# Differential attention: the head norms' sums of squares from split squares, in two passes over a constant tile

## The chip, the cores and the metric

One core of one Trainium2 chip runs the whole program. The metric is the device time of one execution in microseconds (us), lower is better. The engines named below are TensorE (PE; its weight loads are shown as PEld), VectorE (DVE), ScalarE (ACT), GpSimd (POOL) and SyncE (SP). Each takes its instructions from a list of its own, and a semaphore makes one engine wait for another.

## The reference

Two blocks of layers run over 512 positions of width 1024, with 16 meta tokens ahead of them (528 in all). The first block is a stick-breaking attention, an MLP, a differential attention and an MLP; the second holds another attention, a recurrent layer and a mixture of experts. The change lies in the differential attention alone. Its 8 heads have two keys and two queries of 64 rows each and a value of 128 rows, and every one of them, and the output too, goes through a root-mean-square norm:

```python
def rmsnorm(x, g):
    xf = x.astype(jnp.float32)
    y = xf * lax.rsqrt(jnp.mean(xf * xf, axis=-1, keepdims=True) + EPS)
    return (y * g.astype(jnp.float32)).astype(x.dtype)
...
k1 = apply_partial_rope(rmsnorm(kk[..., 0, :], kv_k_norm_g[0]), cos, sin)
q1 = apply_partial_rope(rmsnorm(qq[..., 0, :], b_q_norm_g[j, 0]), cos, sin)
w = probs(q1b, k1f) - lam * probs(q2b, k2f)     # two softmaxes, causal
o = rmsnorm(o, b_subln_g[j]) * (1.0 - lam_init)
h = h + merge_heads(o).astype(h.dtype) @ b_w_o[j]
```

The mean of squares over a head's rows is the sum that the change is about.

## The kernel before

Activations lie with the feature on the partition and the position on the free axis. A dense product in full precision is written as three matmuls of the type F32R, on operands that are split into a high and a low part (`hi*whi`, `lo*whi`, `hi*wlo`; lines 215 to 217). The method `split` (lines 367 to 369) makes such a pair from an fp32 tile: ScalarE copies to the high part, VectorE subtracts it from the tile.

The differential attention works on one head ("pair": its two keys, its two queries) after another, eight in all. Two Python generators are interleaved by `script`. `df_dense` yields the dense products: keys (two halves of 264 columns), queries and values of pair p, and at last a part of the output product. `df_attn` yields the attention of the pairs: scores (`z`, line 867), softmax, the transposes of its weights (`flip`, lines 902 to 907), the product with the values (line 974) and the norm of the output (`tail`, lines 981 to 988). The tables PAT, PAT6 and PAT7 say how many dense steps stand between the steps of the attention; so TensorE's order is written by hand, and the other engines' order is chosen by a scheduler from dependencies and priorities.

A norm runs so. `head_square` (line 749) squares a head's 128 rows on ScalarE into a tile `hsq`. `head_norm` (lines 752 to 764) multiplies `hsq` on TensorE by `blk`, a 128x128 tile with 1/64 in two diagonal blocks, so that the means of both 64-row heads stand on all their rows (line 758: two halves of 264 columns for keys, 512 for queries). `rsqrt` (lines 345 to 357) then needs ScalarE four times (349, 353, 354, 355) and VectorE twice (356, 357). Lines 760 to 764 apply gain and rotary embedding on VectorE, with one product on POOL (line 763). The `due` list in `df_dense` says after how many dense steps the norm of keys and of queries is emitted (DK 4, DQ 1; for the first pair D0). The sums go to the PSUM pool `dn`, of two banks, which the dense products use too. The norm of the output does the same with `osq` (line 979) and `ones_s`, filled with 1/128 (line 983); its result is split into `oT_hi` and `oT_lo`.

The names in rows: `dn`, `z`, `tr`, `o` are PSUM tiles; `wT` holds the transposed weights; `e` the exponentials; `st` the maxima and sums of a softmax; `k` and `dfq`, `dfl` the split keys and queries; `ms` the mean square; `hrs` and `ors` the reciprocal roots.

Of the kernel before, what the change touches and what calls it, by code (L numbers as in the profile page):

```python
# [7 lines left out]
F32 = mybir.dt.float32  # L8
F32R = mybir.dt.float32r
# [10 lines left out]
S = 512  # L20
L = S + NM
# [8 lines left out]
class Net:  # L30
# [682 lines left out]

    def df_setup(self):
        nc, c = self.nc, self.ap
        self.blk = c.tile([128, 128], F32, name="blk")
        nc.vector.memset(self.blk, 0.0)
        for r in (slice(0, 64), slice(64, 128)):
            nc.vector.memset(self.blk[r, r], 1.0 / 64)
        self.ones_s = c.tile([128, 128], F32, name="ones_s")  # L720
        nc.vector.memset(self.ones_s, 1.0 / 128)
        self.rope = c.tile([128, 2, L], F32, name="rope")
        nc.sync.dma_start(self.rope, self.w["rope"])
        self.small = c.tile([128, 3], F32, name="bsmall")
        nc.sync.dma_start(self.small, self.w["b_small"])
        nc.vector.tensor_scalar(self.small[:, 0:1], self.small[:, 0:1], -0.5, None, op0=ALU.mult)
        nc.vector.tensor_scalar(self.small[:, 1:2], self.small[:, 1:2], -0.5 * 0.125, None, op0=ALU.mult)
        lam_init = 0.8 - 0.6 * math.exp(-0.3)
        nc.vector.tensor_scalar(self.small[:, 2:3], self.small[:, 2:3], -0.5 * (1.0 - lam_init), None, op0=ALU.mult)
        lp = c.tile([128, 4, 64], F32, name="lp")  # L730
        src = self.w["b_lambda"]
        nc.sync.dma_start(lp, bass.AP(tensor=src.tensor, offset=src.offset, ap=[[0, 128], [64, 4], [1, 64]]))
        pr = c.tile([128, L], F32, name="hsq", bufs=2)[:, :64]
        lam = c.tile([128, 2], F32, name="lam")
        for i in range(2):
            nc.vector.scalar_tensor_tensor(pr, lp[:, 2 * i, :], 1.0, lp[:, 2 * i + 1, :], op0=ALU.mult, op1=ALU.mult,
                                           accum_out=lam[:, i:i + 1])
        nc.scalar.activation(lam, lam, AF.Exp)
        self.ql = self.lows(c, "dfl", S, 3)
        self.meta_rows(c, 1)  # L740
        self.nlam = c.tile([128, 1], F32, name="nlam")
        nc.vector.tensor_sub(self.nlam, lam[:, 1:2], lam[:, 0:1])
        nc.vector.tensor_scalar(self.nlam, self.nlam, -lam_init, None, op0=ALU.add)
# [3 lines left out]
    def head_square(self, x):  # L747
        sq = self.ap.tile([128, L], F32, name="hsq", bufs=2)[:, :x.shape[1]]
        self.nc.scalar.activation(sq, x, AF.Square)
        return sq  # L750

    def head_norm(self, x, sq, c0, g):

        nc, n = self.nc, x.shape[1]
        rs = self.ap.tile([128, L], F32, name="hrs")[:, :n]
        for a, b in (HALVES if n == L else ((0, n),)):
            ps = self.bank(b - a)
            nc.tensor.matmul(ps, self.blk, sq[:, a:b], start=True, stop=True)
            self.rsqrt(rs[:, a:b], ps, b - a)
        nc.vector.scalar_tensor_tensor(x, x, g, rs, op0=ALU.mult, op1=ALU.mult)  # L760
        nc.vector.stream_shuffle(sq, x, self.SHUF)
        nc.vector.tensor_mul(x, x, self.rope[:, 0, c0:c0 + n])
        nc.gpsimd.tensor_mul(sq, sq, self.rope[:, 1, c0:c0 + n])
        nc.vector.tensor_add(x, x, sq)
# [146 lines left out]
    def df_attn(self, o_pairs):  # L911
        nc, ap = self.nc, self.ap
# [14 lines left out]
        w, tail = {}, None  # L927
# [14 lines left out]
        for p in range(8):  # L942
# [7 lines left out]
            if tail:  # L950
                tail()
# [21 lines left out]
            for i, j in enumerate((4, 0, 1, 2, 3)):  # L973
                nc.tensor.matmul(o[:, 128 * (j % 4):], vn[:, j, :], wT[:, j, 128 * (j % 4):], start=(i == 0),
                                 stop=(i == 4), skip_group_check=True)
            of = ap.tile([128, S], F32, name="of", bufs=2)
            nc.scalar.activation(of, o, AF.Copy)
            sq = ap.tile([128, S], F32, name="osq")
            nc.scalar.activation(sq, of, AF.Square)

            def tail(p=p, of=of, sq=sq):
                pn = self.bank()
                nc.tensor.matmul(pn, self.ones_s, sq, start=True, stop=True)
                rs = ap.tile([128, S], F32, name="ors")
                self.rsqrt(rs, pn, S)
                nc.vector.scalar_tensor_tensor(of, of, gain, rs, op0=ALU.mult, op1=ALU.mult)
                self.split(of, *o_pairs[p][:2])
                self.outs = p + 1
        yield self.END[0]
        tail()  # L990
        yield self.END[1]

# [1166 lines left out]
```

## Time and profile before

| | |
|---|---|
| median of 3 runs | 2514.88 us (2513.75 to 2515.01) |
| profiled execution | 2519.67 us, of which the span is 2517.9 us |
| granted TensorE clock, mean | 0.987 of full speed |
| PE busy | 2425.6 us, 96% of the span |
| DVE busy | 1449.4 us, 58% |
| ACT busy | 1167.3 us, 46% |
| POOL busy | 164.8 us, 7% |
| differential attention | from about 720 to 990 us of the span |
| one pair in its steady part | 29.75 us (a pair's first key sum at 777.25, the next at 807.02) |

The busy shares are means over the program; within a stage the waits tell more. A row of a timeline gives the start, the duration, the engine, the line, the tiles, the number of instructions, and in brackets the idle time ahead of it and what ended it. A matmul's duration holds its way through the array, so successive starts tell what it occupies.

### The profile page before, as it was taken

To read this page: it belongs to the slowest core of one execution; us is meant where nothing else is said; L and a number is where in the kernel's file an instruction comes from. 1 tells how busy PE (TensorE), PEld (TensorE's weight loads), DVE (VectorE), ACT (ScalarE), POOL (GpSimd) and SP (SyncE) were. 2 spreads that over 40 slices of the span, in tenths; PEclk is the share of its full clock that TensorE was granted. 3 is DMA by queue.
4 is the path that set the end of the run, shared out by engine and by line. 5 is a ranking of instruction groups with operands and counts; after the bars stand their busy time and mean duration, and the time that the engine had idled before them with its cause. 6 is when DMAs were issued, how large, how long until landed. Compare 5 with 4: busy or idle time off the path is not lost. (4 is left out here: it accounts for less than half of the span.)

```text
span 2517.9 us, 38327 instructions
## 1 busy us (share of the span) xinstructions
PE 2425.6 (96%) x14656; PEld 1937.2 (77%) x14656; DVE 1449.4 (58%) x2744; ACT 1167.3 (46%) x2271; POOL 164.8 (7%) x169
## 2 busy tenths in 40 slices
PE   8999988999999999999999999999999989999996
PEld 8999988999988887788887888999888733344332
DVE  6666686443457776533445658899654544344434
ACT  6777653332447776422334666555653322222222
POOL 0000055000001110000000000000000111000000
PEclk9999999999999999999999999999999889999998
DMA  3111299333342223333334212222245799997996
GB/s 119 51 51 35 69 343 378 122 93 88 102 154 101 101 101 97 105 97 92 94 99 120 73 57 62 68 59 64 80 129 205 282 380 409 408 401 300 408 407 240
DMA packets 126986, 418.26 MB, mean 166 GB/s; under 512 B 16464, under 2 KB 20816, under 8 KB 126800
## 3 DMA queue, kind: packets, MB, share of 16 engines
q1 hardware_dynamic: 116288, 382.22, 43.2%
q0 software_dynamic: 9936, 31.47, 3.2%
q8 instruction: 116, 1.90, 0.3%
q10 hardware_dynamic: 576, 2.10, 0.2%
q14 instruction: 70, 0.57, 0.1%
HBM read 386.83 MB, written 33.62 MB: 167 GB/s over the span
## 5 line engine op out<-in xcount | busy, mean ns | idle before, releaser
L215 PE MATMUL dn<-hg_hi,whi 128*128 128x264 f32 (+1 forms) x1616 | 525.0, 325 | 8.7 <-ACT hg_hi L336 6.9
L182 ACT ACTIVATE whi<-wraw 128x1024 fp32r<-128x1024 f32 (+1 forms) x261 | 259.1, 993 | 551.1 <-PE dn L216 266.1
L217 PE MATMUL dn<-hg_hi,wlo 128*128 128x264 f32 (+1 forms) x1616 | 511.2, 316 | 3.0 <-DVE wlo L183 3.0
L216 PE MATMUL dn<-hg_lo,whi 128*128 128x264 f32 (+1 forms) x1616 | 510.7, 316 | 2.1 <-DVE hg_lo L337 2.0
L183 DVE TENSOR_TENSOR wlo<-wraw,whi 128x1024 fp32r<-128x1024 f32 (+1 forms) x261 | 300.1, 1150 | 77.4 <-ACT whi L182 75.9
L215 PEld LDWEIGHTS dn<-hg_hi,whi 128*128 128x128 f32 x1616 | 308.2, 191 | 30.1 <-ACT hg_hi L336 6.9
L216 PEld LDWEIGHTS dn<-hg_lo,whi 128*128 128x128 f32 x1616 | 308.0, 191 | 24.1 <-DVE hg_lo L337 4.3
L217 PEld LDWEIGHTS dn<-hg_hi,wlo 128*128 128x128 f32 x1616 | 307.9, 191 | 21.5 <-DVE wlo L183 3.3
L1839 PE MATMUL b<-ew,X 128*64 128x512 f32 (+1 forms) x964 | 236.4, 595 | 3.2 <-DMA ew<-e_in 3.1
L1839 PEld LDWEIGHTS b<-ew,X 128*64 128x64 f32 (+1 forms) x964 | 77.1, 138 | 150.9 <-issue 122.4
L217 PE MATMUL mb<-hg_hi,wlo 128*128 128x264 f32 (+1 forms) x504 | 163.1, 324 | 7.3 <-DVE wlo L183 7.3
L217 PE MATMUL mb<-rhi,wlo 128*128 128x264 f32 (+1 forms) x512 | 164.6, 321 | 0.4 <-DVE wlo L183 0.4
L215 PE MATMUL mb<-rhi,whi 128*128 128x264 f32 (+1 forms) x512 | 164.6, 322 | 0.0
L216 PE MATMUL mb<-rlo,whi 128*128 128x264 f32 (+1 forms) x512 | 164.4, 321 | 0.0
L216 PE MATMUL mb<-hg_lo,whi 128*128 128x264 f32 (+1 forms) x504 | 161.9, 321 | 0.0
L215 PE MATMUL mb<-hg_hi,whi 128*128 128x264 f32 (+1 forms) x504 | 161.8, 321 | 0.0
L1074 DVE SCALAR_TENSOR_TENSOR H<-b,lsg 128x512 f32<-128x512 f32 x17 | 11.7, 691 | 216.2 <-ACT lsg L1073 216.2
L1866 PE MATMUL b<-ew,HT 128*64 128x512 f32 (+1 forms) x476 | 116.2, 604 | 3.3 <-ACT X L1827 3.3
L1071 ACT ACTIVATE lsg<-b 128x512 f32<-128x512 f32 x17 | 10.2, 597 | 226.4 <-PE b L1839 226.4
L217 PEld LDWEIGHTS mb<-hg_hi,wlo 128*128 128x128 f32 x504 | 95.4, 189 | 14.9 <-DVE wlo L183 7.9
L217 PEld LDWEIGHTS mb<-rhi,wlo 128*128 128x128 f32 x512 | 96.5, 188 | 7.9 <-DVE wlo L183 0.6
L216 PEld LDWEIGHTS mb<-rlo,whi 128*128 128x128 f32 x512 | 96.7, 189 | 7.4
(532 smaller groups left out, 5051.7 us busy)
## 6 DMA issues: line engine op xcount, KB each, us to landing
ew<-e_in SPq DMA_DIRECT2D x233, 512.0 KB, 10.1
ew<-e_out SPq DMA_DIRECT2D x108, 512.0 KB, 10.1
wraw<-mlp_in SPq DMA_DIRECT2D x64, 512.0 KB, 3.6
wraw<-mlp_out SPq DMA_DIRECT2D x64, 512.0 KB, 3.7
wraw<-w SPq DMA_DIRECT2D x60, 512.0 KB, 3.6
wraw<-a_qkv SPq DMA_DIRECT2D x24, 512.0 KB, 3.6
preh<-phi POOLq DMA_DIRECT2D x24, 512.0 KB, 5.4
prel<-plo POOLq DMA_DIRECT2D x24, 512.0 KB, 7.1
```

Of the source, the lines that this page charges most:

```text
L182: nc.scalar.activation(hi, raw, AF.Copy)
L183: nc.vector.tensor_sub(lo, raw, hi)
L215: nc.tensor.matmul(ps, whi[:, k, :], hi[:, a:b], start=(k == 0), stop=False)
L216: nc.tensor.matmul(ps, whi[:, k, :], lo[:, a:b], start=False, stop=False)
L217: nc.tensor.matmul(ps, wlo[:, k, :], hi[:, a:b], start=False, stop=(k == len(act) - 1))
L1071: nc.scalar.activation(t, x, AF.Abs)
L1074: nc.vector.scalar_tensor_tensor(out, x, 0.0, t, op0=ALU.min, op1=ALU.subtract)
L1839: nc.tensor.matmul(ps[r], X[:, k, r], w[k][:, c:c + 512], start=(k == 0), stop=(k == KT - 1), skip_group_check=True)
L1866: nc.tensor.matmul(ys[c][r], HT[:, k, r], w[k][:, c * 512:c * 512 + 512], start=(k == 0), stop=(k == 3), skip_group_check=True)
```

## The change

The constants `blk` and `ones_s` become tiles of type F32R. A new method `parts` splits a tile of squares into `sqh` and `sql`, by ScalarE (high) and VectorE (low), and `sums` multiplies the constant by both and adds them up in the bank, so that two single-pass matmuls stand where one fp32 matmul stood (in the trace each of those shows as two records). `sqh` and `sql` have one buffer each, shared by keys, queries and outputs. The order in which the generators are interleaved is as before.

```diff
     def df_setup(self):
-        self.blk = c.tile([128, 128], F32, name="blk")
-        nc.vector.memset(self.blk, 0.0)
+        self.blk = c.tile([128, 128], F32R, name="blk")
+        nc.vector.memset(self.blk.bitcast(F32), 0.0)
...
-        self.ones_s = c.tile([128, 128], F32, name="ones_s")
-        nc.vector.memset(self.ones_s, 1.0 / 128)
+        self.ones_r = c.tile([128, 128], F32R, name="ones_s")
+        nc.vector.memset(self.ones_r.bitcast(F32), 1.0 / 128)
...
     def head_square(self, x):
         sq = self.ap.tile([128, L], F32, name="hsq", bufs=2)[:, :x.shape[1]]
         self.nc.scalar.activation(sq, x, AF.Square)
-        return sq
+        return sq, self.parts(sq)
+
+    def parts(self, sq):
+        hi, lo = (self.ap.tile([128, L], F32R, name="sq" + nm)[:, :sq.shape[1]] for nm in "hl")
+        self.split(sq, hi, lo)
+        return hi, lo
+
+    def sums(self, ps, w, parts, a, b):
+        for i, x in enumerate(parts):
+            self.nc.tensor.matmul(ps, w, x[:, a:b], start=(i == 0), stop=(i == 1))
 
     def head_norm(self, x, sq, c0, g):
+        sq, parts = sq
...
-            nc.tensor.matmul(ps, self.blk, sq[:, a:b], start=True, stop=True)
+            self.sums(ps, self.blk, parts, a, b)
...
             sq = ap.tile([128, S], F32, name="osq")
             nc.scalar.activation(sq, of, AF.Square)
-            def tail(p=p, of=of, sq=sq):
+            parts = self.parts(sq)
+            def tail(p=p, of=of, parts=parts):
                 pn = self.bank()
-                nc.tensor.matmul(pn, self.ones_s, sq, start=True, stop=True)
+                self.sums(pn, self.ones_r, parts, 0, S)
```

The rows below are instructions in the order of one engine: line, operation, output, inputs, shape. Lines behind 750 stand some 11 further down in the changed kernel.

VectorE, second pair, where its queries' squares are split. The kernel before has this piece of its list:

```order
L760 SCALAR_TENSOR_TENSOR xf<-xf,bsmall,hrs 128x528
L894 RECIPROCAL st<-st 128x2
L924 SCALAR_TENSOR_TENSOR e<-e,st 128x144
L922 TENSOR_SCALAR st<-st,nlam 128x1
L252 SCALAR_TENSOR_TENSOR xf<-dn,rstd 128x264
L924 SCALAR_TENSOR_TENSOR e<-e,st 128x272
L761 STREAM_SHUFFLE hsq<-xf 128x528
L907 COPY wT_8586<-tr 16x128
```

The changed kernel has at the same place:

```order
L771 SCALAR_TENSOR_TENSOR xf<-xf,bsmall,hrs 128x528
L891 TENSOR_REDUCE st<-z 128x2
L905 RECIPROCAL st<-st 128x2
L772 STREAM_SHUFFLE hsq<-xf 128x528
L933 TENSOR_SCALAR st<-st,nlam 128x1
L773 TENSOR_TENSOR xf<-xf,rope 128x528
L905 RECIPROCAL st<-st 128x2
L935 SCALAR_TENSOR_TENSOR e<-e,st 128x144
L933 TENSOR_SCALAR st<-st,nlam 128x1
L775 TENSOR_TENSOR xf<-xf,hsq 128x528
L935 SCALAR_TENSOR_TENSOR e<-e,st 128x272
L369 TENSOR_TENSOR sql<-hsq,sqh 128x512
```

The low part of the second pair's queries (`sql`) stands behind the keys' rotary embedding of that pair, whose last step (L775) takes the product that POOL makes of the shuffled `hsq`.

VectorE, a steady pair, around the norm of the output of the pair before it. The kernel before:

```order
L378 TENSOR_TENSOR k_9391<-xf,k_9391 64x528
L252 SCALAR_TENSOR_TENSOR xf<-dn,rstd 128x264
L378 TENSOR_TENSOR k_9392<-xf,k_9392 64x528
L880 TENSOR_REDUCE st<-z 128x2
L356 TENSOR_TENSOR sq<-ms,sq 128x512
```

The changed kernel:

```order
L252 SCALAR_TENSOR_TENSOR xf<-dn,rstd 128x264
L378 TENSOR_TENSOR k_9429<-xf,k_9429 64x528
L378 TENSOR_TENSOR k_9430<-xf,k_9430 64x528
L891 TENSOR_REDUCE st<-z 128x2
L369 TENSOR_TENSOR sql<-osq,sqh 128x512
L356 TENSOR_TENSOR sq<-ms,sq 128x512
```

The low part of the output's squares comes behind both key subtractions and the maximum of the 400-column scores.

ScalarE, a steady pair, around the queries' squares. The kernel before:

```order
L354 ACTIVATE hrs<-hrs 128x264
L353 ACTIVATE hrs<-ms 128x264
L355 ACTIVATE sq<-hrs 128x264
L354 ACTIVATE hrs<-hrs 128x264
L355 ACTIVATE sq<-hrs 128x264
L906 COPY wT_8586<-o 128x4x128
```

The changed kernel:

```order
L354 ACTIVATE hrs<-hrs 128x264
L353 ACTIVATE hrs<-ms 128x264
L355 ACTIVATE sq<-hrs 128x264
L354 ACTIVATE hrs<-hrs 128x264
L368 ACTIVATE sqh<-hsq 128x512
L355 ACTIVATE sq<-hrs 128x264
L917 COPY wT_8586<-o 128x4x128
```

The high part of the queries' squares stands two instructions ahead of the copy that the product with the values takes.

## Rows read from the trace of the kernel before

**Rows 1.** The page's first part: busy time, share and instructions of each engine.

```profile
PE 2425.6 (96%) x14656; PEld 1937.2 (77%) x14656; DVE 1449.4 (58%) x2744; ACT 1167.3 (46%) x2271; POOL 164.8 (7%) x169
```

**Rows 2.** Groups by line, 690 to 990 us: busy, mean ns | idle before, releaser.

```profile
L758 PE MATMUL dn<-hsq,blk 128*128 128x264 f32 (+1 forms) x48 | 19.4, 487 | 5.4 <-ACT ms L349 3.4 <-DVE xf L252 2.0
...
L983 PE MATMUL dn<-osq,ones_s 128*128 128x512 f32 x16 | 8.4, 605 | 0.0
...
L369 DVE TENSOR_TENSOR oT_lo<-of,oT_hi 128x512 fp32r<-128x512 f32 x7 | 4.8, 692 | 0.1
L368 ACT ACTIVATE oT_hi<-of 128x512 fp32r<-128x512 f32 x7 | 4.4, 629 | 4.2 <-DVE of L986 4.2
```

**Rows 3.** Waits of PE, 690 to 990 us: total us, times, longest us.

```profile
PE dn L758 <- ACT ms L349: 3.4, 7, 0.5
PE o L974 <- DVE wT L907: 2.2, 6, 0.4
...
PE z L867 <- ACT dfq L396: 1.9, 3, 0.7
```

**Rows 4.** Windows: length, busy of PE, PEld, DVE, ACT, POOL; granted clock, DMA, GB/s.

```profile
353.00:356.00 3.00, 2.36 (x14) 2.36 (x15) 2.04 (x4) 2.97 (x5) 0.98 (x2) 0.76 0.97 362
...
753.00:755.00 2.00, 2.00 (x8) 1.00 (x7) 1.88 (x6) 1.97 (x8) 0.00 (x0) 0.73 0.00 0
755.00:758.00 3.00, 3.00 (x17) 2.95 (x16) 2.03 (x8) 2.67 (x9) 0.00 (x0) 0.61 0.03 5
810.00:840.00 30.00, 29.16 (x190) 25.15 (x189) 22.69 (x51) 22.63 (x54) 3.26 (x2) 1.00 0.30 109
```

**Rows 5.** Timeline of PE in a steady pair: start, duration, instruction, [idle before].

```profile
811.86 3.25 PE L974 MATMUL o<-wT,vn 128*128 128x512 f32 x10 [0.36 <-DVE wT L907]
...
819.92 1.02 PE L983 MATMUL dn<-osq,ones_s 128*128 128x512 f32 x2
820.78 0.38 PE L902 MATMUL o<-ident,e 128*128 128x128 f32 x2
...
830.05 0.40 PE L215 MATMUL dn<-hg_hi,whi 128*128 128x512 f32 x1
830.29 0.39 PE L216 MATMUL dn<-hg_lo,whi 128*128 128x512 f32 x1
```

**Rows 6.** Timeline of ACT in the same pair.

```profile
810.92 0.57 ACT L906 COPY wT<-o 128x512 f32<-128x512 f32 x1
...
816.84 1.31 ACT L377 ACTIVATE k<-xf 64x528 fp32r<-64x528 f32 x2
```

**Rows 7.** Timeline of DVE in the same pair.

```profile
816.10 0.71 DVE L764 TENSOR_TENSOR xf<-xf,hsq 128x528 f32<-128x528 f32 x1 [1.08 <-POOL hsq L763]
816.72 0.50 DVE L924 SCALAR_TENSOR_TENSOR e<-e,st 128x272 f32<-128x272 f32 x1
...
819.35 0.98 DVE L880 TENSOR_REDUCE st<-z 128x2 f32<-128x800 f32 x1
820.36 0.69 DVE L356 TENSOR_TENSOR sq<-ms,sq 128x512 f32<-128x512 f32 x1
```

**Rows 8.** Timelines of PE, DVE and POOL in the second pair.

```profile
753.52 1.71 PE L758 MATMUL dn<-hsq,blk 128*128 128x512 f32 x2
...
755.52 0.76 DVE L760 SCALAR_TENSOR_TENSOR xf<-xf,bsmall,hrs 128x528 f32<-128x528 f32 x1
...
759.43 1.32 POOL L763 TENSOR_TENSOR hsq<-hsq,rope 128x528 f32<-128x528 f32 x1 [10.60 <-DVE wT L907]
```

**Rows 9.** Timelines of PE and ACT at the last output norm.

```profile
984.03 1.13 PE L983 MATMUL dn<-osq,ones_s 128*128 128x512 f32 x2
984.40 0.58 ACT L851 ACTIVATE part<-dn 128x512 f32<-128x512 f32 x1
...
991.22 0.49 PE L215 MATMUL dn<-oT_hi,whi 128*128 128x512 f32 x1 [1.03 <-ACT oT_hi L368]
```

**Rows 10.** Timeline of PE, a long wait in the first layer.

```profile
353.64 0.39 PE L217 MATMUL dn<-hg_hi,wlo 128*128 128x264 f32 x1 [3.04 <-DVE wlo L183]
```

More of the change, by code (lines that the diff above doesn't have):

```diff
@@ L715, in df_setup @@
         nc, c = self.nc, self.ap
-        self.blk = c.tile([128, 128], F32, name="blk")
-        nc.vector.memset(self.blk, 0.0)
+        self.blk = c.tile([128, 128], F32R, name="blk")
+        nc.vector.memset(self.blk.bitcast(F32), 0.0)
         for r in (slice(0, 64), slice(64, 128)):
-            nc.vector.memset(self.blk[r, r], 1.0 / 64)
-        self.ones_s = c.tile([128, 128], F32, name="ones_s")
-        nc.vector.memset(self.ones_s, 1.0 / 128)
+            nc.vector.memset(self.blk[r, r].bitcast(F32), 1.0 / 64)
+        self.ones_r = c.tile([128, 128], F32R, name="ones_s")
+        nc.vector.memset(self.ones_r.bitcast(F32), 1.0 / 128)
         self.rope = c.tile([128, 2, L], F32, name="rope")
```

## The prediction

> **What bounds the kernel now.** The page's first part comes first: TensorE (PE) is busy for 96% of the span, no other engine for over 58% [rows 1]. So time is won where PE gets less to do, and lost where PE must wait. The change lies between 720 and 990 us, so the windows come next: in 30 us of a steady pair PE is busy for 29.16 us at the full clock, while VectorE (DVE) and ScalarE (ACT) have 22.7 each [rows 4]. The other two engines are thus three quarters full, and what they still have free lies in waits of their own, not in one piece. Third, PE's waits of the stage: the sums wait seven times for the copy that frees a bank (3.4 us together), the product with the values six times for a transposed weight (2.2 us), the scores three times for doubled queries (1.9 us) [rows 3]. Nothing of PE's waits for the squares themselves, but for one long one at the start. Last, the timelines tell at which moment PE reaches a sum, and what ACT and DVE do at that moment.
>
> **What the change removes.** There are 8 pairs, and each has two key sums of 264 columns, a query sum and an output sum of 512. An output sum starts at 819.92 and the next matmul at 820.78: 0.86 us. A single pass over 512 columns takes 830.29 - 830.05 = 0.24 us (0.23 between its neighbours, which I use) [rows 5]. Two of them are 0.46, so 0.40 us is saved for 512 columns, and by width some 0.20 for 264. Per pair that is 0.20 + 0.20 + 0.40 + 0.40 = 1.2 us, and 9.6 us in all, as much as the two groups' 19.4 + 8.4 us of busy time, about a third [rows 2]. All of it lies on PE and would come out of the end if nothing waited.
>
> **What it adds.** 24 copies on ACT and 24 subtractions on DVE, three of each per pair. The nearest rows are the split of the output, of the same kind and width: 0.63 us on ACT, 0.69 on DVE [rows 2]. That is 1.9 us and 2.1 us per pair of 29.75 us, on engines with 7 us free in that time [rows 4], so neither becomes the bound by its sum. What decides is where they stand in the lists, since the second matmul of each sum now waits for the subtraction. I take it sum by sum.
>
> *Keys, steady pair.* High and low part come right behind the square, where ACT and DVE have nothing urgent; PE reaches the sums later. Gain 0.3 us for both halves. But ACT makes the high part of the queries ahead of the copy of `wT` that the values' product waits for (810.92; PE waits 0.36 for it at 811.86 [rows 5, 6]). The square that is split is ready by then, so the copy moves back by somewhat under the 0.63 us of such a copy [rows 2], of which the earlier sums give back the most: the product starts at about 811.9, 0.04 later than before. The keys' gain is gone into that wait.
>
> *Queries, steady pair.* Their low part stands right behind the keys' roots on DVE, about 3 us before PE reaches the sum: gain 0.40, so PE comes to the output sum about 0.36 early, at 819.56.
>
> *Output, steady pair.* Here the low part stands behind both key subtractions and the maximum over 800 columns, that is, at the place of the instruction that starts at 820.36 behind the maximum from 819.35 [rows 7]. What stands ahead of it is what stood there before; the keys come from a product that waits for POOL (816.10, [rows 7]) and their copies on ACT start at 816.84 [rows 6]. So the subtraction runs from 820.36 to 821.05, and with 0.3 us for the second matmul the sum ends at about 821.35, against 820.78. PE waits for some 1.3 us from its early arrival, and the pair ends 0.57 later than before. There are five such sums (790.0 to 909.1): 5 x 0.57 = +2.85 us. Behind PE in its list stand the transposes of the next weights and the dense products; nothing passes them. In the sixth pair the low part stands ahead of the maximum: the same walk gives -0.29. In the seventh it stands behind a split of the weights and gives +0.64.
>
> Here a rule of the Trainium skill bears on the sum (Perfetto Trace Analysis, section Tensor Engine Instruction (MATMUL, LD_WEIGHTS)): DVE and ACT take their instructions strictly in order, PE alone can bring some weight loads forward. The trace agrees: the scaling of `e` at 816.72 stands behind a product that waited 1.08 us for POOL, although its own input had been ready [rows 7]. If they could overtake, the low part would run as soon as its high part is there, before 820, and all five sums would gain 0.40 instead of losing; that is the second rival below.
>
> *The last output sum.* PE is at 984.03, right behind the square [rows 9]. ACT has a weight split and the copy that starts at 984.40 and takes 0.58 [rows 9] ahead of the high part: it runs from about 984.9 to 985.5, the low part to 986.2, the sum to 986.5, against 984.9 before. All of the chain to the end of the stage is exposed, since PE waits there for the output's split (1.03 us at 991.22 [rows 9]): +1.5 us.
>
> *The second pair's queries, at the start.* PE reaches this sum at 753.52, and with the clock at half it ended at about 755.2 [rows 8]. In the changed order the low part stands behind the last step of the keys' rotary embedding. The gain step stood at 755.52 (0.76 us) [rows 8]; it moves forward by about 0.6, then come the shuffle (0.74) and POOL's product, 1.3 to 1.7 us (1.32 in the trace [rows 8]), so the embedding ends near 758.6, a scaling of `e` takes to 759.0, and the subtraction 0.69: 759.7. PE then stands for some 5 us at this sum: +4.9. Set against it: the twelve matmuls behind it ran at half the clock before (granted 0.61 from 755 to 758 [rows 4]), which gives 1.0 back; a wait of 0.74 for doubled queries falls away, one of those in [rows 3]; the bank costs 0.1. Net about +3.25 us. The first pair's gain of 0.7 is used up by a wait for the low part of the second pair's keys.
>
> *Clock.* A wait of 3.04 us at 353.64 was followed by a granted clock of 0.76 from 353 to 356 [rows 4, 10]; from 753 to 758 the same lower level (1.2 GHz against 2.4) was granted for 0.27 x 2 x 2 + 0.39 x 2 x 3 = 3.4 us, behind waits of this stage's start [rows 4]. A stretch of 3.4 us at half costs up to 1.7 us, where PE has work. Such a fall behind the 5 us stand is likely, I put +0.9 for it.
>
> The Trainium skill (TensorE: Matmul & The Clock Gate, Part 1) says the same more strictly: behind enough idleness TensorE goes to half its clock, and only activity releases it. No row here shows what the shorter waits that I expect would do; if the rule takes them in, the third rival comes.
>
> **The sum.** 3.25 + 0.9 + 2.85 - 0.29 + 0.64 + 1.5 = +8.85 us. The profiled execution took 2519.67 us around its span of 2517.9, which is 4.8 above the median of the runs, 2514.88; it would take 2528.5. On the median the forecast is 2523.7 us. Nothing outside the stage changes its order, so the difference passes to the end unless a wait there swallows it.
>
> The bounds of the unknown: no row of before shows PE waiting for a split of squares. From below the wait is nothing, and all of 9.6 us is won: 2505.3. From above, each of eight pairs pays 1.3 us at the output sum and 0.5 to 0.7 at others with no gain anywhere (+14.4 to +16), and the start +5: about 2535. I take the walk's value, which stands nearer to the upper rows.
>
> **Rivals.**
> 1. *The waits and the gains cancel.* The scheduler's places are as I read them, but DVE reaches them earlier than I think, for instance because the maximum over the scores starts with the earlier PE. If the output sum waits 0.6 us less in all pairs (-4) and the start 2 us less, +8.85 becomes about +2.5: 2517.4. For it: each wait of mine rests on differences of some tenths. Against it: what stands ahead of the low part at 820.36 is bound by POOL and ACT, not by PE [rows 7].
> 2. *The gain comes out, faster.* All low parts are ready when PE comes: -9.6, 2505.3; with the start's wait alone left it would be -9.6 + 4 = about 2509. For it: DVE and ACT have 7 us free per pair [rows 4]. Against it: they work in order, and the low part stands behind a maximum that ends at 820.3 while PE is there at 819.6.
> 3. *The clock falls in the steady pairs too.* Each pair would then have a wait of 1.3 us at the output sum, and if 3.4 us at half follow in five to eight of them, 1.7 us each comes on top of the forecast: +8.5 to +13.6, and 2532 to 2537. For it: the falls behind waits in [rows 4, 10]. Against it: the wait there was longer (3.04 us [rows 10]), and the waits that a steady pair has now leave the clock at 1.00 [rows 4].
>
> **How the numbers follow.** About 0.2% (5 us) is what a measurement of this kernel can tell from no change, so slower begins at 2519.9 and faster ends at 2509.9. The forecast has 0.58, the third rival 0.10, the first 0.19, the second 0.13. The forecast's own spread (some 4 us, from eight waits of tenths and one of 5 us) stays above 2519.9 but for a little, which goes with part of the first rival's upper side: slower 0.67, same 0.20, faster 0.13. The range goes from 2510 to 2531: it leaves out the second rival and most of the third.
>
> **What would show it.** In the profile of the changed kernel: 64 matmuls of the sums at 0.23 (512) and 0.12 us (264) from start to start; PE waits for `sql` of DVE at five output sums of about 1.3 us each, one of some 5 us at the second pair's query sum; a pair's period of 30.3 instead of 29.75 us; the last output sum ending about 1.5 us later behind its square. The prediction is wrong if the output sums show no wait for `sql`, if the period falls below 29.4, or if the stage before its first steady pair takes no longer than before.

## The result: slower by half a per cent, and the profile after

The changed kernel takes 2526.45 us (median of 6 runs, 2523.64 to 2530.69), the kernel before 2514.70 us on the same chip (6 runs, 2511.63 to 2515.60). The ratio is 1.0053, its 95% interval 1.0043 to 1.0063: 11 to 16 us slower. The forecast was 2523.7 us, with 2510 to 2531 as its range.

The profiled execution took 2524.61 us, with a span of 2522.8. What lies ahead of the stage ran 6 us faster in it than in the profile of before (the first key sum stands at 727.31 against 733.31), with the same instructions in the same order. So two executions are compared from that sum on, and not by their spans.

The page's first part (it answers to [rows 1]): PE is busy for 13.5 us less, DVE for 32 us more, ACT for 11 us more, and the span is longer all the same. Of PE's 13.5 us, 6.6 lie ahead of the stage, in the part that ran faster, and 3.9 in the stage (246.3 us before, 242.4 now, from the first key sum to the first matmul that takes the last output's split). Of DVE's, 27.5 lie in the stage: the 24 subtractions make some 16.6 of them (0.69 each), and the rest goes with two kinds of instruction that were there before and take longer now (the product `xf` times `rope`, 18.7 us added up against 11.5, and the scaling of `e`, 25.3 against 18.9; successive instructions overlap a little, so busy time grows by less).

```profile
PE 2412.1 (96%) x14656; PEld 1927.5 (76%) x14656; DVE 1481.5 (59%) x2768; ACT 1178.5 (47%) x2295; POOL 162.8 (6%) x169
```

The waits of PE from 690 to 1000 us (total us, times, longest; it answers to [rows 3]). The first and the fifth row are new: 13.5 us for low parts, 2.2 us for high parts. The waits for a freed bank (`ms`), a transposed weight (`wT`) and doubled queries (`dfq`) have each grown by 0.6 to 1.2 us; the wait of 2.0 us at the second pair's key sum (<-DVE xf L252 in [rows 2]), the long one at the start, is gone. The prediction has it among waits for squares, but it was for a bank: the first half's sum had run on the same squares at 745.74.

```profile
PE dn L760 <- DVE sql L369: 13.5, 10, 5.2
PE dn L760 <- ACT ms L349: 4.6, 8, 0.6
PE o L985 <- ACT wT L917: 3.1, 5, 0.6
PE z L878 <- ACT dfq L396: 2.5, 2, 1.8
PE dn L760 <- ACT sqh L368: 2.2, 3, 1.5
```

PE's timeline of the steady pair that answers to [rows 5]; the pair's first key sum starts at 807.55, as it starts at 807.02 in the profile of before. The sum of the output is reached at 820.27, 12.72 us behind that start (12.90 before). Its second matmul waits 1.28 us, and the next matmul starts at 822.38, 14.83 us behind (13.76 before).

```profile
808.55 0.39 PE L760 MATMUL dn<-sqh,blk 128*128 128x264 f32 x1 [0.60 <-ACT ms L349]
...
812.36 3.28 PE L985 MATMUL o<-wT,vn 128*128 128x512 f32 x10 [0.61 <-ACT wT L917]
...
820.27 0.50 PE L760 MATMUL dn<-sqh,ones_s 128*128 128x512 f32 x1
...
822.04 0.50 PE L760 MATMUL dn<-sql,ones_s 128*128 128x512 f32 x1 [1.28 <-DVE sql L369]
822.38 0.38 PE L913 MATMUL o<-ident,e 128*128 128x128 f32 x2
```

DVE in the same pair (it answers to [rows 7]). The third fence is of ACT. The low part of the output's squares starts at 821.30 behind the maximum, in the place that the forecast gave it, but 13.75 us behind the pair's start and not 13.34. POOL's product (the second fence) runs from 815.50 to 817.30. The high part ends at 820.22, just ahead of the first matmul.

```profile
816.02 1.58 DVE L935 SCALAR_TENSOR_TENSOR e<-e,st 128x272 f32<-128x272 f32 x1
817.52 0.69 DVE L775 TENSOR_TENSOR xf<-xf,hsq 128x528 f32<-128x528 f32 x1
...
820.29 0.98 DVE L891 TENSOR_REDUCE st<-z 128x2 f32<-128x800 f32 x1
821.30 0.69 DVE L369 TENSOR_TENSOR sql<-osq,sqh 128x512 fp32r<-128x512 f32 x1
```

```profile
815.50 1.80 POOL L774 TENSOR_TENSOR hsq<-hsq,rope 128x528 f32<-128x528 f32 x1 [17.58 <-DVE st L933]
```

```profile
819.59 0.63 ACT L368 ACTIVATE sqh<-osq 128x512 fp32r<-128x512 f32 x1
```

The second pair (it answers to [rows 8]): PE, then DVE, then windows with the granted clock in the column behind POOL, the last of them a stretch of steady pairs (it answers to the one of 30 us in [rows 4]). PE waits 5.19 us for the low part of the queries, which ends at 754.39. The clock has fallen to half (0.50, that is 1.2 GHz) ahead of that wait, between 748 and 749 us, behind shorter waits (4.1 us in four of them from 739 to 747), and it is at half until between 758 and 759.

```profile
745.53 0.33 PE L878 MATMUL z<-k,dfq 128*128 128x144 f32 x1 [1.79 <-ACT dfq L396]
...
754.45 0.80 PE L760 MATMUL dn<-sql,blk 128*128 128x512 f32 x1 [5.19 <-DVE sql L369]
```

```profile
741.87 1.49 DVE L773 TENSOR_TENSOR xf<-xf,rope 128x512 f32<-128x512 f32 x1
...
752.68 0.69 DVE L775 TENSOR_TENSOR xf<-xf,hsq 128x528 f32<-128x528 f32 x1
753.30 0.49 DVE L935 SCALAR_TENSOR_TENSOR e<-e,st 128x272 f32<-128x272 f32 x1
753.71 0.68 DVE L369 TENSOR_TENSOR sql<-hsq,sqh 128x512 fp32r<-128x512 f32 x1
```

```profile
748.00:751.00 3.00, 0.92 (x3) 0.28 (x1) 3.00 (x9) 2.37 (x10) 0.28 (x1) 0.56 0.00 0
751.00:754.00 3.00, 0.00 (x0) 0.00 (x0) 3.00 (x7) 1.34 (x3) 1.47 (x1) 0.50 0.00 0
754.00:758.00 4.00, 3.56 (x16) 3.38 (x16) 1.90 (x4) 3.18 (x6) 0.00 (x0) 0.50 0.02 4
...
810.00:840.00 30.00, 27.45 (x181) 24.00 (x180) 26.55 (x54) 22.92 (x54) 3.38 (x2) 1.00 0.26 95
```

The last output (it answers to [rows 9]): its sum waits for both parts, and the wait for the output's split behind it is longer too.

```profile
991.65 0.50 PE L760 MATMUL dn<-sqh,ones_s 128*128 128x512 f32 x1 [1.49 <-ACT sqh L368]
992.38 0.50 PE L760 MATMUL dn<-sql,ones_s 128*128 128x512 f32 x1 [0.23 <-DVE sql L369]
...
998.94 0.50 PE L215 MATMUL dn<-oT_hi,whi 128*128 128x512 f32 x1 [1.16 <-ACT oT_hi L368]
```

### The profile page after: what moved, and what is told of

The parts are those of the page before. It is cut to its first block, busy times and chain, and to the rows that moved or that the text cites. A ratio compares the mean times of both kernels' runs of the same rounds, so it can differ in the third digit from the quotient of the medians.

```text
span 2522.8 us, 38380 instructions
## 1 busy us (share of the span) xinstructions
PE 2412.1 (96%) x14656; PEld 1927.5 (76%) x14656; DVE 1481.5 (59%) x2768; ACT 1178.5 (47%) x2295; POOL 162.8 (6%) x169
## 5 line engine op out<-in xcount | busy, mean ns | idle before, releaser
L215 PE MATMUL dn<-hg_hi,whi 128*128 128x264 f32 (+1 forms) x1616 | 517.8, 320 | 8.3 <-ACT hg_hi L336 6.2
L215 PEld LDWEIGHTS dn<-hg_hi,whi 128*128 128x128 f32 x1616 | 306.0, 189 | 27.5 <-ACT hg_hi L336 6.2
```

The source lines that it names most:

```text
L215: nc.tensor.matmul(ps, whi[:, k, :], hi[:, a:b], start=(k == 0), stop=False)
```

## The experiments

Each profile is cut at four starts on PE: the first key sum of the first, third and eighth pair, and the first matmul that takes the last output's split. That gives the start, five pairs (their mean stands in the table) and the end. In the profile of before the four starts are 733.31, 777.25, 926.02 and 991.22. The ratio is that of the runs to runs of before on the same chip, with its 95% interval.

| kernel | start | one pair | end | stage against before | ratio |
|---|---|---|---|---|---|
| before | 43.94 | 29.75 | 65.20 | | |
| changed kernel | 49.43 | 30.81 | 68.13 | +13.7 | 1.0053 (1.0043 to 1.0063) |
| e1_no_low: no low parts | 44.09 | 30.18 | 66.92 | +4.0 | 1.0006 (0.9998 to 1.0015) |
| e2_out_only: outputs alone | 43.93 | 30.40 | 67.89 | +5.9 | 1.0018 (1.0009 to 1.0027) |
| e3_heads_only: keys and queries alone | 48.96 | 29.36 | 65.22 | +3.1 | 1.0018 (1.0009 to 1.0028) |
| e4_prio: splits with priority | 45.41 | 29.58 | 66.89 | +2.3 | 1.0006 (0.9996 to 1.0016) |
| e5_from_pair2: heads from the third pair on | 42.99 | 29.52 | 65.19 | -2.1 | 0.9997 (0.9988 to 1.0005) |
| e6_single: one pass, nothing added | 43.04 | 29.59 | 66.42 | -0.5 | 1.0001 (0.9992 to 1.0011) |
| e7_rope_dve: rotary product on DVE | 50.61 | 29.63 | 67.59 | +8.5 | 1.0046 (1.0033 to 1.0059) |
| e8_keys_out: keys and outputs | 44.24 | 30.88 | 68.36 | +9.1 | 1.0038 (1.0025 to 1.0051) |
| e9_mix: e5 and early outputs | 43.94 | 29.88 | 65.47 | +0.9 | 1.0002 (0.9993 to 1.0011) |
| e10_norm_prio: norms with priority | 46.89 | 31.68 | 69.45 | +16.8 | 1.0066 (1.0052 to 1.0079) |
| e10b_mix_prio: e9 and that priority | 43.55 | 32.55 | 65.58 | +14.0 | 1.0046 (1.0033 to 1.0060) |
| e12_before_prio: before and that priority | 43.25 | 31.03 | 65.82 | +6.3 | 1.0028 (1.0016 to 1.0041) |

The stage's difference in one profile and the ratio times 2514 us agree within 4 us in every row, so the stage holds the difference. A start can differ by 1 us between profiles of the same code, by the clock alone (e5_from_pair2 shows it).

**e1_no_low.** In `parts`:

```diff
-        hi, lo = (self.ap.tile([128, L], F32R, name="sq" + nm)[:, :sq.shape[1]] for nm in "hl")
-        self.split(sq, hi, lo)
-        return hi, lo
+        hi = self.ap.tile([128, L], F32R, name="sqh")[:, :sq.shape[1]]
+        self.nc.scalar.activation(hi, sq, AF.Copy)
+        return hi, hi
```

Expected: 

> The changed kernel without the 24 low parts: both matmuls of a sum read the high part, so the means of squares come out near twice too large; PE's work is that of the change, ACT's 24 copies stay, VectorE has none of the subtractions. Theory (the loss is PE's waits for the low part, placed late on VectorE): no wait for sql, the start 4 to 5 us shorter than in the changed kernel, the period of a steady pair at about 29.2 to 29.4 us instead of 30.81 (before 29.77), the last output sum still waits 1.5 us for sqh; about 2508 us, 0.2 to 0.4% below before. Rival (the two single passes or ACT's copies cost more than they save, or the clock): the time stays at 2520 us or more.

The rival fell: 10 us of the 13 go with the subtractions, and the start is as before. But the pair takes 30.18 us and not 29.2 to 29.4, and the time is 2516.9 us and not 2508. PE's rows show it 0.81 us ahead of before at the end of the output sum, and then a wait that was not there: the evacuation that frees its bank (L252 on DVE) stands behind a product that takes 1.72 us.

```profile
829.63 0.51 PE L215 MATMUL dn<-hg_hi,whi 128*128 128x512 f32 x1 [0.93 <-DVE xf L252]
```

```profile
826.03 1.72 DVE L773 TENSOR_TENSOR xf<-xf,rope 128x512 f32<-128x512 f32 x1
...
829.15 0.42 DVE L252 SCALAR_TENSOR_TENSOR xf<-dn,rstd 128x264 f32<-128x264 f32 x1
```

```profile
825.63 1.57 POOL L774 TENSOR_TENSOR hsq<-hsq,rope 128x512 f32<-128x512 f32 x1 [10.07 <-DVE hsq L772]
```

POOL runs its own product from 825.63 to 827.20, and the DVE instruction that starts within it ends 0.55 us behind POOL's end. e7_rope_dve tests that.

**e2_out_only and e3_heads_only.** `head_square` returns the fp32 tile in the first, the outputs keep it in the second, and `sums` gets the old way:

```diff
+        if not isinstance(parts, tuple):
+            self.nc.tensor.matmul(ps, w.bitcast(F32), parts[:, a:b], start=True, stop=True)
+            return
...
-        return sq, self.parts(sq)           # e2_out_only
+        return sq, sq
...
-            parts = self.parts(sq)          # e3_heads_only
+            parts = sq
```

Expected of the first: 

> Only the output's squares are split; keys and queries keep the fp32 matmul. If the output sum's loss is the place of its own low part behind the maximum alone, the wait at the output sum is about 1 us, the period about 30.3 us (29.77 + 0.57), the start as before, the end +2.9 us: about +6 us, 2520 us. If the queries' low part, ahead of the keys' rotary embedding, makes the other 0.4 to 0.5 us of the changed kernel's +1.04 per pair, then this kernel shows +0.57 and not +1.04. If the queries' low part has no part in it, the period is 30.6 us or more.

Expected of the second: 

> Only the keys' and queries' squares are split; the output keeps the fp32 matmul. Start: +5.5 us as in the changed kernel. Steady pair: the output sum does not wait for VectorE, so the gain of the sums less the later copy of wT comes out: 29.77 - 0.2 to - 0.6, about 29.4 us, -2 us over five pairs. End as before. Sum about +3.5 us, 2518 us. If the start's loss were a matter of the output's split, it would be as before and the time 2512 us.

Both came out as the theory has it. Outputs alone: the wait is 0.77 us, the pair 30.40 (0.65 more than before; 0.57 in the forecast), the start as before. Heads alone: 5.0 of the start's 5.5 us, a pair of 29.36, the end as before. The parts do not add up in the pair: +0.65 and -0.39 give +0.26, and the change as a whole shows +1.06. DVE's rows show why. With the heads split, the maximum ahead of the output's place starts 12.72 us behind the pair's first sum (the last row below, of e3, where that sum is at 803.66), as in the changed kernel (12.74), and not at 12.31 as in e2 or 12.33 as before. In e3 no output sum waits for what stands behind it; with the outputs split too, their low part comes 0.41 us later, which with e2's 0.65 gives the 1.06.

```profile
817.45 0.40 PE L763 MATMUL dn<-sqh,ones_s 128*128 128x512 f32 x1
818.62 0.50 PE L763 MATMUL dn<-sql,ones_s 128*128 128x512 f32 x1 [0.77 <-DVE sql L369]
```

```profile
816.38 0.98 DVE L894 TENSOR_REDUCE st<-z 128x2 f32<-128x800 f32 x1
```

**e4_prio.**

```diff
-        self.split(sq, hi, lo)
+        with self.tc.high_priority(offset=self.AHEAD):
+            self.split(sq, hi, lo)
```

Expected: 

> The change with both halves of each split under the priority offset that the softmax has (300). The scheduler then puts the low part of the second pair's queries ahead of the keys' embedding and the low part of each output ahead of the key subtractions and the maximum. Theory of the place: the 5.2 us wait at the start falls below 1 us, the waits at the five output sums from 1.27 to under 0.3 us, the period to about 29.4 us; the last output sum +0.7 us; about 2511 us, 0.1 to 0.2% below before. Rival (VectorE and ScalarE have no room for the splits wherever they stand): other waits take their place and the period stays above 30.3 us.

The theory of the place holds: all waits for `sql` together are 1.1 us and not 13.5, and 11 us of the loss are gone. `sqh` and `sql` have one buffer each here too, so it was not the lack of a second buffer that made the waits. The pair, at 29.58, is not the 29.4 expected, nor the time, 2515.2 us, the 2511: other waits have grown, for a bank (`ms`) and for the evacuation, as these rows of PE's waits show. At the start the wait for doubled queries is 2.83 us.

```profile
PE dn L761 <- ACT ms L349: 5.7, 8, 0.8
PE z L879 <- ACT dfq L396: 3.1, 2, 2.8
PE dn L215 <- DVE xf L252: 2.2, 5, 0.4
...
PE dn L761 <- DVE sql L369: 1.1, 3, 0.5
```

**e5_from_pair2.** With `sums` as in e2:

```diff
+        return sq, self.parts(sq) if on else sq
...
-            self.head_square(kf)
+            self.head_square(kf, p > 1)    # and qf; the split only then
...
-            parts = self.parts(sq)          # outputs
+            parts = sq
```

Expected: 

> Keys' and queries' squares are split from the third pair on; the first two pairs and all outputs keep the fp32 matmul. If the parts add up, the time from the first key sum of the first pair to that of the third is 43.9 us as before (49.4 in the changed kernel), a steady pair takes 29.36 us, the end is as before: 2.0 us less than before in the stage, about 2512.9 us. If the start's 5.5 us were not the second pair's low part but something that the first split in the stage brings with it, it moves to the third pair and the stage takes 3 us more than before.

The sum is met, -2.1 us in the stage against -2.0, but by luck. The start is 0.95 us shorter than before, though nothing is changed in its two pairs: the clock did not fall in this execution (windows below, before first; e9_mix, with the same sums there, has 0.93 and 43.94 us again). The five pairs gave only 1.2 us of the 2.0: the first of them has a longer wait for a bank, the other four take 29.35 us each, as expected. That the start's loss does not move to the third pair holds. The ratio, 0.9997, does not tell it from before.

```profile
740.00:763.00 23.00, 19.85 (x114) 16.94 (x113) 18.18 (x38) 15.69 (x39) 4.58 (x3) 0.93 0.26 92
```

```profile
740.00:763.00 23.00, 19.17 (x137) 17.23 (x136) 20.32 (x45) 16.55 (x42) 3.03 (x2) 1.00 0.25 92
```

**e6_single.**

```diff
-        self.nc.scalar.activation(sq, x, AF.Square)
-        return sq, self.parts(sq)
+        hi = self.ap.tile([128, L], F32R, name="sqh", bufs=2)[:, :x.shape[1]]
+        self.nc.scalar.activation(hi, x, AF.Square)
+        return sq, (hi,)
```

The output's squares are written as F32R in the same way.

Expected: 

> ScalarE writes the squares as F32R at once; one single-pass matmul sums them, with no copy and no subtraction added: the squares' low parts are left out of the sums. PE has 0.64 us less for 512 columns and 0.33 for 264, 1.9 us per pair, 15 us in all. If PE bounds the stage alone, the period falls to 27.8 us and the time to 2500 us. If the gain is given back at the next bank or at the next transposed weight (as the kernel without low parts gave back 1.1 of its 0.8 us per pair behind an evacuation on VectorE), the period stays at 29.0 us or more, and the trace shows new waits for the evacuation (xf of line 252) or for wT and ms: 2508 to 2512 us.

The second case holds, but for the time, 2513.7 us: 1.9 us less work per pair leave 0.16 us. The wait for `ms` takes 0.24 (0.72 against 0.48). Behind the output sum PE is still 1.65 us ahead of before; the scores behind it take 0.3, and the evacuation of the row below 1.1. The wait for `wT`, 0.34, is that of before (0.36). The order of DVE's list has changed again, though nothing was added to it.

```profile
826.15 0.50 PE L215 MATMUL dn<-hg_hi,whi 128*128 128x512 f32 x1 [0.92 <-DVE xf L252]
```

**e7_rope_dve.**

```diff
-        nc.gpsimd.tensor_mul(sq, sq, self.rope[:, 1, c0:c0 + n])
+        nc.vector.tensor_mul(sq, sq, self.rope[:, 1, c0:c0 + n])
```

Expected: 

> The changed kernel with the product of the shuffled tile and the rotary table on VectorE instead of POOL (16 instructions). Theory: a VectorE product of two tiles that begins while POOL runs its own takes till POOL ends (1.71 us instead of 0.69 in the changed kernel). Then the product xf times rope takes 0.70 us on the mean instead of 1.21, the scaling of e 0.55 instead of 0.83, and VectorE pays 0.7 per product for it; the wait at the second pair's query sum falls from 5.2 to under 4.5 us, the period below 30 us; about 2516 us. Rival: the 1.7 us are the instruction's own at that place (its operands or its wait), and stay.

The long instructions are gone with POOL's: groups by line from 776 to 930 us, the changed kernel first, then this one.

```profile
L935 DVE SCALAR_TENSOR_TENSOR e<-e,st 128x144 f32<-128x144 f32 (+3 forms) x20 | 16.6, 829 | 0.0
L773 DVE TENSOR_TENSOR xf<-xf,rope 128x528 f32<-128x528 f32 (+1 forms) x10 | 12.1, 1211 | 0.0
```

```profile
L935 DVE SCALAR_TENSOR_TENSOR e<-e,st 128x144 f32<-128x144 f32 (+3 forms) x21 | 11.5, 549 | 0.0
L773 DVE TENSOR_TENSOR xf<-xf,rope 128x528 f32<-128x528 f32 (+1 forms) x10 | 6.9, 695 | 0.0
```

The pair falls below 30 us as expected, but since this order has the low part ahead of the key subtractions too, that does not tell which of the two did it. The time is missed by 8 us (2524.0): the wait at the second pair's queries is now 3.28 us for the high part and 2.35 for the low, and its keys wait 2.93.

**e8_keys_out.** With `sums` as in e2:

```diff
+        return sq, self.parts(sq) if on else sq
...
-            sq = self.head_square(qf)
+            sq = self.head_square(qf, False)
```

Expected: 

> Keys' and outputs' squares are split, the queries' sum stays fp32. If the queries' low part, in the list ahead of the keys' embedding, makes the difference between the changed kernel's +1.06 per pair and the +0.64 that the output's split alone costs, the period is 30.4 us here too, with the output sum's wait longer than the 0.78 us of the output's split alone by at most the keys' 0.3 us. If the keys' low part makes it, the period is 30.8 us as in the changed kernel. Start: the second pair's key sum waits about 1 us, its query sum does not wait: 44 to 45 us. Time about 2520 us.

My reading was wrong: without any low part of the queries the pair takes 30.88 us, and the wait is 1.73. With the outputs split, the keys' split is enough to bring the extra loss. The rows of DVE and POOL in this kernel show how: POOL's product starts 0.24 us later than in e2, counted from the pair's first key sum (7.54 against 7.30), and the scaling of `e` now stands ahead of the last embedding step, starts within POOL's product (812.14 to 813.93) and lasts to 814.23. In e2, the same scaling stands behind that step and takes 0.49 us.

```profile
812.66 1.57 DVE L938 SCALAR_TENSOR_TENSOR e<-e,st 128x272 f32<-128x272 f32 x1
814.15 0.69 DVE L778 TENSOR_TENSOR xf<-xf,hsq 128x528 f32<-128x528 f32 x1
```

```profile
812.14 1.79 POOL L777 TENSOR_TENSOR hsq<-hsq,rope 128x528 f32<-128x528 f32 x1 [17.10 <-DVE st L936]
```

```profile
813.62 0.71 DVE L778 TENSOR_TENSOR xf<-xf,hsq 128x528 f32<-128x528 f32 x1 [1.08 <-POOL hsq L777]
814.25 0.49 DVE L938 SCALAR_TENSOR_TENSOR e<-e,st 128x272 f32<-128x272 f32 x1
```

From the pair's first key sum, the embedding step stands at 9.07 us in e2 and at 9.55 in e8, and the output's low part at 13.32 and 13.79.

**e9_mix, e10_norm_prio, e10b_mix_prio and e12_before_prio.** The first adds to e5 the outputs of the first five pairs, split under priority:

```diff
             parts = sq
+            if p < 5:
+                with self.tc.high_priority(offset=self.AHEAD):
+                    parts = self.parts(sq)
```

The others put the norms' last five steps under priority, in the changed kernel, in e9 and in the kernel before:

```diff
+        with self.tc.high_priority(offset=self.AHEAD):
             nc.vector.scalar_tensor_tensor(x, x, g, rs, op0=ALU.mult, op1=ALU.mult)
...
             nc.vector.tensor_add(x, x, sq)
```

Expected of e9_mix: 

> Keys and queries split from the third pair on, and the outputs of the first five pairs split with the priority of the softmax, so that their low part stands ahead of the key subtractions; the last three outputs stay fp32. If the place of the low part is all that costs at the output sum, no wait for sql there and the period falls from 29.36 (heads alone) to 29.0 us: stage 3.5 us shorter than before, 2511.4 us. If the time won at the output sum is given back at the next bank, as in the kernel without low parts, a wait for the evacuation (xf of line 252) of about 0.4 us follows and the period stays at 29.3 to 29.4 us.

Expected of e10_norm_prio: 

> The changed kernel with the five last steps of the head norms (gain, shuffle, three steps of the rotary embedding) under the softmax's priority. In the order, the second pair's low part of the queries now stands ahead of the keys' embedding: the 5.2 us wait goes, the start falls from 49.4 to 45 to 46 us. In the steady pairs the part of VectorE's list ahead of the output's low part is the same as in the changed kernel: the wait for it stays at 1.2 to 1.3 us and the period at 30.8 us. End as in the changed kernel. About 2522 us.

Expected of e10b_mix_prio: 

> The kernel e9_mix with that priority of the norms' last steps: the queries' embedding moves ahead on VectorE, so that its product xf times rope no longer falls into POOL's (mean 0.70 instead of 1.2 us) and the evacuation behind it comes earlier. If that evacuation is what gives the gain back, its wait goes and the period is 28.9 to 29.0 us: stage 4 to 5 us shorter than before, 2510.5 us, 0.2% below before. If not, another wait (ms, wT) takes it and the period stays at 29.3 us.

Expected of e12_before_prio: 

> The kernel before with that priority of the norms' last steps, as a control: PE's work is that of before, its waits in a steady pair are 0.48 and 0.37 us, so no more than 0.4 us per pair can come out of it; period 29.4 to 29.8 us, time within 2 us of before. If it gains as much as e10b_mix_prio, the split has no part in that gain.

e9 shows its second case and more: no wait for `sql` at the outputs, 0.27 us for the evacuation, 0.83 for a bank, and a pair of 29.88. e10 takes the 5.2 us wait away as expected and leaves 1.28 us at the outputs as expected, but the start only falls to 46.9, a new wait of 0.6 us comes at the evacuation, and the pair takes 31.68 and not 30.8. e10b (14 us slower than expected) and e12 (7 us slower than before, where no more than 2 were expected) refute the idea behind them: with the embedding moved ahead, the evacuation of line 252 stands behind it, and PE waits 2.2 to 2.3 us per pair in e10b and 1.0 in e12, where nothing was split at all.

```profile
825.63 0.39 PE L215 MATMUL dn<-hg_hi,whi 128*128 128x264 f32 x1 [2.30 <-DVE xf L252]
```

```profile
826.31 0.39 PE L215 MATMUL dn<-hg_hi,whi 128*128 128x264 f32 x1 [1.00 <-DVE xf L252]
```

In e10b something comes on top that the forecast of the change had among its rivals: the clock falls to half in three of the five steady pairs, behind the waits of 2.2 to 2.3 us. These pairs take 33.0 us (the first of them 33.8, with a longer wait for a bank too), the two between them 31.5. The windows are its third and fourth pair, with the granted clock as in [rows 4].

```profile
770.50:804.33 33.83, 29.56 (x186) 26.34 (x185) 26.59 (x55) 24.52 (x59) 3.08 (x2) 0.95 0.25 94
804.33:835.80 31.47, 27.97 (x186) 24.77 (x185) 26.38 (x54) 23.65 (x56) 3.08 (x2) 1.00 0.28 101
```

No kernel tried is shown to be faster than the one before.

## Why the prediction was right, and where its terms were off

| term | forecast | measured in the profile |
|---|---|---|
| start, to the third pair, with the clock | +3.25, and +0.9 for the clock | +5.5 |
| five steady pairs | +2.85 | +5.3 |
| sixth output | -0.29 | +0.3 |
| seventh output | +0.64 | +1.0 |
| last output | +1.5 | +1.7 |
| sum | +8.85 | +13.7 |

(The last three outputs' lines come from the starts of like matmuls in both profiles, counted from the eighth pair's first key sum: some 0.3 us later than before behind the sixth output, some 1.25 behind the seventh, 2.93 at the end.)

Every line came out dearer than forecast, so no misses cancelled. The mechanism was right, and but for the sixth output the direction of each line; the forecast's sum is two thirds of what was measured. At the sixth output, where the walk gave a gain, PE waits 0.37 us for the low part.

*What was saved.* As forecast: behind the keys PE is 0.29 us ahead of before, behind the queries 0.41. The later copy of `wT` takes the keys' gain back (a wait of 0.61 against 0.36), so PE comes to the output sum 0.18 us before its old place, where 0.36 was forecast: the high part, behind the two key copies on ACT, is not there sooner (820.22). These copies start at 818.25, behind an embedding that is late too (next paragraph), and started at 816.84 before.

*The wait for the low part of the outputs.* The mechanism is shown by e2 (outputs alone bring +0.65), e3 (without them the pair gains 0.39) and e4 (with the low part ahead, the wait is gone). The wait's length was forecast, 1.3 us, and is 1.27 to 1.28, but that agreement is luck: from the start of the first matmul to the end of the subtraction the forecast has 1.49 us (819.56 to 821.05) and the profile 1.72 (820.27 to 821.99), and the profile counts the idle time from the end of a first matmul of 0.50. The cost per pair was forecast as 0.57 us and is 1.06. What failed is the sentence that what stands ahead of the low part is what stood there before. The change moved that too: the maximum ahead of it starts 12.74 us behind the pair's first sum, and 12.33 before. Two causes stand in DVE's rows, the queries' low part (0.67 us) ahead of the second half's roots of the keys, where the forecast had it behind them, and the scaling of `e`, which now starts within POOL's product. Counted from the pair's first sum, POOL's product starts 0.66 us later than before (7.96 against 7.30) and the last embedding step 0.89 later (9.97 against 9.08); the evacuation of line 252, which stood between the key subtractions, now fills a wait ahead of both, and so 0.47 comes back. e8 shows that a delay of this size does not need the queries' low part. What the pair would lose with one of the two causes alone stays open, since no run has queries and outputs split without the keys.

*A second rule should have been weighed.* In the changed kernel POOL's product runs from 815.50 to 817.30, and the scaling of `e` that starts at 816.02 ends at 817.60. In the kernel before, the DVE product of the same pair began 0.13 us ahead of POOL's and took 0.71 (two fences, DVE and POOL):

```profile
814.19 0.71 DVE L762 TENSOR_TENSOR xf<-xf,rope 128x528 f32<-128x528 f32 x1
```

```profile
814.32 1.74 POOL L763 TENSOR_TENSOR hsq<-hsq,rope 128x528 f32<-128x528 f32 x1 [19.03 <-DVE st L894]
```

The Trainium skill (SBUF — State Buffer, section Who interferes with whom) says that a DVE instruction with two inputs in SBUF and a GpSimd instruction that reads SBUF shut each other out for the whole instruction, and that the order of issue decides who waits. The trace agrees in both cases, and e7 shows the long instructions gone with POOL's product. The forecast charged POOL's product only to the step that takes its result. In the stage of the changed kernel 15 DVE instructions with two SBUF inputs start within one of POOL's products, and 2 in the kernel before.

*The start.* Its place and its cause are shown by e2 (keys and queries not split: 43.93), e5 (not in the first two pairs: 42.99) and e4 (the low part ahead: 45.41). The wait was forecast as some 5 us and is 5.19. The size missed 1.3 us in all. Followed along like matmuls from the first key sum, PE is 0.80 us ahead of before behind the second pair's key sums and 0.60 late when it comes to the query sum, where the forecast had it level: the first pair's doubled queries let it wait 1.79 us (0.39 before), and their embedding took 1.49 us beside POOL's product. Behind the query sum it is 6.0 late. The forecast's two terms of the clock, 1.0 had back and 0.9 lost, nearly cancel; here the clock was at half for some 4 us behind the wait, and PE is 6.6 late when it is back at full. The wait for doubled queries (0.74 us, at 774.88 before) falls away as forecast, which leaves 5.5. The fall itself came ahead of the long wait (748 to 749), and not behind it as the forecast has it.

*The rivals.* The waits and gains did not cancel, and the gain did not come out. The clock stayed at 1.00 in the steady pairs (810 to 840, and in the whole of 776 to 931), with a wait of 1.28 us in each, so the third rival fell as well. In e10b, with waits of 2.2 to 2.3 us, the clock did fall, and such a pair took some 1.5 us more than its neighbours.

*The range.* The profile's sum, +13.7, and the ratio, +13.3 us, lie above the forecast's +8.85, and inside the range up to 2531.

## What to carry to other kernels

Work that is taken off the engine that bounds the span and given to others is worth only what its consumers don't wait for: ask of each added instruction where it stands in its engine's list, and what the instructions ahead of it wait for in turn. Where a scheduler orders those engines, one added instruction also reorders its neighbours, so the old trace tells their durations but not their places. Where one of the neighbours is a product on POOL, ask which instructions of VectorE will start within it. And when PE gets ahead, look at the next bank or operand: of 1.9 us less work per pair 1.1 were given back at one evacuation.

## What the runs showed of the hardware

A DVE instruction of two SBUF tiles that started while POOL multiplied two such tiles ended 0.3 to 0.55 us behind POOL's end: 1.57 to 1.72 us for work that takes 0.49 to 0.71 otherwise. In all profiles with products on POOL the time behind POOL's end goes by the width, 0.30 us for 272 columns, 0.43 for 400, 0.55 for 512, so that little or nothing of such an instruction seems to have run beside POOL. A DVE maximum over scores in PSUM is not lengthened: in e3, two of them that start within POOL's product (820.59 to 822.12) take what they take elsewhere, some 0.7 us each.

```profile
820.88 1.31 DVE L901 TENSOR_REDUCE st<-z 128x1 f32<-128x528 f32 x2
```

An fp32 sum over 512 columns occupied PE for 0.86 us, and a pass on F32R tiles 0.23; behind a wait for an operand the next matmul started 0.34 us after the one that had waited (822.04, 822.38), and not 0.23.
